# Attention scores in one-bank pieces from the top, products one step later, two transposed banks, and two gates halved

## The chip, the cores and the metric

The kernel runs on one core of a Trainium2 chip. The time is that of the device, in microseconds (us), from start to end of one launch; three runs of the kernel before gave 1307.58, 1307.06 and 1303.7, with the median at 1307.06. PE is the TensorE matrix engine, DVE is VectorE, ACT is ScalarE, POOL is GpSimd and SP is SyncE.

## What is computed

One layer of an encoder trunk on a sequence of 1024 tokens with 1024 channels, all in float32. Two token mixers (a pooling mixer over u and a stick-breaking attention over q, k, v) are merged by sigmoid gates, then an MLP with squared ReLU follows. The part on which the change bears:

```python
h = rmsnorm(x) * g_pre_mix
[u_pool | q | k | v] = h @ w_in
y_pool = multiscale_pool(u_pool) @ w_br_pool
y_sb   = stick_breaking_attention(q, k, v) @ w_br_sb       # 8 heads of 64
[g_pool | g_sb] = sigmoid(h @ w_gate + b_gate)
x = x + rmsnorm((g_pool * y_pool + g_sb * y_sb) @ w_out) * g_post_mix
x = x + rmsnorm(relu(rmsnorm(x) * g_pre_mlp @ w_up)**2 @ w_down) * g_post_mlp

def stick_breaking_attention(q, k, v):        # for each block of 128 queries t
    z = (qb @ kb.T) * scale
    mask = s < t                               # strictly causal
    log_1mb = where(mask, log_sigmoid(-z), 0)
    tail = cumsum(log_1mb, from the right) - log_1mb
    attn = where(mask, exp(log_sigmoid(z) + tail), 0)
    out = attn @ vb
```

So A[t,s] is sigmoid(z[t,s]) times the product of sigmoid(-z[t,j]) over all j between s and t.

## The kernel before, in words

**Precision.** A product of two float32 matrices is done as three matmuls of their high and low parts (hi x hi, lo x hi, hi x lo). `L112`, `L113` and `L114` are these three; a "dense step" is such a triple for one block of 128 input channels.

**The stages.** The input phase computes the two halves of the tokens' mean squares (`ms`, by a matmul with ones, L332), turns them into reciprocal roots `rb` (`rstd`: Ln L153 and Exp L154 on ACT, then L155 to L157 on DVE), transposes `rb` on PE (`rt`, L336) and copies a column of it into `rcol` (L337). Beside this run the products of u (`du`, `zu`: four groups, two halves each; L380 multiplies a finished half by `rb` and so frees its bank), the pooling mixer (`dm`), q and k of the first heads, and the first half of v. Then come attention, the merge of the branches, and the MLP.

**Attention.** Eight heads; each has eight rows of 128 queries, done in the order 6, 7, 4, 5, 2, 3, 0, 1. `att_scores` does one row i, which is w = 128(i+1) keys wide: the scores z on PE (L544, L547), T = sigmoid(z) and F = sigmoid(-z) on ACT (L551, L552), POOL zeroes T above the diagonal (L554), DVE replaces F by its running product from the right (the scan, L559) and multiplies T by it (L560). `att_out` does a pair of rows g: for each of its g+1 steps m, PE transposes four 128x128 blocks of T (`at`, L576), ACT rounds them to `ahi` (L583), DVE keeps the rest in `alo` (L584), and PE multiplies v by both into `o` (L589). At the end of the pair ACT and DVE add up the two halves of `o` into `oT` (L593, L594).

**What sets the order.** Each engine runs its instructions in a fixed order. `fill` lists, for each head, dense work that is put between the rows and steps (gates `dg`, later q and k `dqk`, the second half of v `dv`): `pump` hands out dense steps by a credit, `w_out` after each step's transpositions and a share of the rest after each row. A gate has two halves of 8 steps, so head 4 has 32 dense steps, heads 5 and 6 have 48 each. Within this, the framework's scheduler orders the instructions, and `marks` pin some of them. Head h's pair g is transposed while the next pair's scores are made.

**Banks.** The accumulators of PE lie in 8 banks: two for dense work (`d`), two tiles of two banks for z (a row of up to 1024 scores), one for `o` and one for `at`. `ms` of the first half and both `rt` use the bank of `at`, `ms` of the second half that of `o`.

Of the kernel before, what the change touches and what calls it, by code (L numbers as in the profile page):

```python
# [29 lines left out]
P = 128  # L30
# [19 lines left out]
class Block:  # L50
# [118 lines left out]
    def build(self):  # L169
# [9 lines left out]
            3: [("q", 2), ("k", 2), ("v", 12, 32)],  # L179
            4: [("g", 3), ("g", 11)],  # L180
            5: [("q", 3), ("k", 3), ("g", 4)],
            6: [("g", 12), ("g", 5), ("g", 13)],
            7: [("g", 6), ("g", 14), ("g", 7)],
# [64 lines left out]
    def phase_in(self):  # L248
# [81 lines left out]
        def stats(h):  # L330
            ms = self.zps.tile([P, H], F32, name="ms", tag="at" if h == 0 else "o", bufs=1)
            nc.tensor.matmul(ms, self.ones, accs[h], start=True, stop=True)  # L332
            self.rstd(ms, pa, ("sq", 3), out=self.rb[h])
            rt = self.zps.tile([P, H], F32, name="rt", tag="at", bufs=1)
            for j in range(4):
                nc.tensor.transpose(rt[:, j * P : j * P + P], self.rb[h][:, j * P : j * P + P], self.eye)  # L336
            nc.vector.tensor_copy(  # L337
                self.rcol[:, 4 * h : 4 * h + 4].rearrange("p (j o) -> p j o", o=1),
                rt.rearrange("p (j o) -> p j o", o=P)[:, :, 0:1],
            )  # L340

        z0 = self.zps.tile([P, 1024], F32, name="zu0", tag="z", bufs=2)
        z1 = self.zps.tile([P, 1024], F32, name="zu1", tag="z", bufs=2)
        d2 = [self.dps.tile([P, H], F32, name="du", tag="d") for _ in range(2)]
        dst = [d2] + [[z[:, h * H : h * H + H] for h in range(2)] for z in (z0, z1)]
        gens = [self.dense_steps(dst[g][0], self.weights(("u", g), 0), self.hT[0]) for g in range(3)]
# [60 lines left out]
        def pool_mix(g, cur):  # L407
# [6 lines left out]
            for h in range(2):  # L414
                c = slice(h * H, h * H + H)
                d = self.zps.tile([P, H], F32, name="dm", tag=("o", "at")[h], bufs=1)
                self.mm3(d, [(wmh[:, g, :], wml[:, g, :], ph[:, c], pq[:, c])])
# [110 lines left out]
    def att_scores(self, h, i):  # L528

        nc = self.nc
        p, j = h // 2, h % 2
        q, qs, k = self.qk[("q", p)][j], self.qk[("qs", p)][j], self.qk[("k", p)][j]
        w = (i + 1) * P
        z = self.zps.tile([P, 1024], F32, name="z", tag="z", bufs=2)
        pieces = [(0, max(256, min(H, w)))]
        if w > H:  # L540
            pieces.append((H, max(256, w - H)))
        tt = slice(i * P, i * P + P)
        for c, n in pieces:
            m = nc.tensor.matmul(z[:, c : c + n], q[:, tt], k[:, c : c + n], start=True, stop=False)  # L544
            if c == 0:
                self.marks.append(m)
            nc.tensor.matmul(z[:, c : c + n], qs[:, tt], k[:, c : c + n], start=False, stop=True)  # L547
        odd = i // 2 % 2
        tl = self.tp.tile([P, 1024 if odd else 768], F32, name="T", tag=f"T{odd}", bufs=2)
        f = self.tp.tile([P, 1024], F32, name="F", tag="F", bufs=1)  # L550
        nc.scalar.activation(tl[:, :w], z[:, :w], AF.Sigmoid)  # L551
        nc.scalar.activation(f[:, :w], z[:, :w], AF.Sigmoid, scale=-1.0)  # L552
        fr = f[:, w - 1 :: -1]
        nc.gpsimd.affine_select(  # L554
            out=tl[:, w - P : w], in_=tl[:, w - P : w], pattern=[[-1, P]], compare_op=ALU.is_gt, fill=0.0, base=0,
            channel_multiplier=1,
        )
        past = self.past[:, 1024 - w :][:, ::-1]
        nc.vector.tensor_tensor_scan(fr, fr, past, 1.0, ALU.mult, ALU.max)  # L559
        nc.vector.tensor_mul(tl[:, : w - 1], tl[:, : w - 1], f[:, 1:w])  # L560
        return tl

    def att_out(self, h, g, a):

        nc = self.nc
        o = self.zps.tile([P, 256], F32, name="o", tag="o", bufs=1)
        hd = (h % 4) * P
        for m in range(g + 1):
            diag = m == g
            at = self.zps.tile([P, H], F32, name="at", tag="at", bufs=1)  # L570
            hi = self.tp.tile([P, H], F32R, name="ahi", tag="ahi", bufs=2)
# [12 lines left out]
            nc.vector.tensor_sub(lo[:, c0:], at[:, c0:], hi[:, c0:].bitcast(F32))  # L584
            for part in (hi, lo):
                for s, c in ((2 * m + 1, 0), (2 * m, 256)):
                    v = self.v[(h // 4, s)].rearrange("p h x -> p (h x)")[:, hd : hd + P]
                    first = m == 0 and c == 0 and part is hi
                    t = nc.tensor.matmul(o, v, part[:, c : c + 256], start=first, stop=diag and c == 256 and part is lo)  # L589
            self.marks.append(t)  # L590
        b = 64 * (h % 2)
# [21 lines left out]
    def phase_attention(self):  # L613
# [5 lines left out]
        self.credit, self.queue = 0.0, []  # L619
        self.w_out = 2.3  # L620
        self.pin = True
        self.cut = 512
# [32 lines left out]
        self.w_out = 8.0  # L655
        self.att_out(*prev)
        while self.queue:
            self.advance()
# [645 lines left out]
```

## Time and profile before

| | before |
|---|---|
| runs | 1307.58, 1307.06, 1303.7 us |
| profiled execution | 1308.59 us |
| its span (first to last instruction) | 1306.8 us |
| attention, by its `at` and `o` rows | about 97 to 502 us |
| mean granted clock of PE | 0.993 |

A row of the timeline reads: start, duration, engine, line, operation, what it writes and reads, shape, how many were merged, and in brackets how long the engine stood idle before it and what ended the wait. A window's row reads: the stretch, its length, then for PE, PE's weight loads, DVE, ACT and POOL the busy time and number of instructions, then PE's granted clock as a share, the DMA engines' busy share and GB/s. Rows of groups end in the busy time, the mean duration in ns, and the idle time before them.

### The profile page before, as it was taken

The page shows a single profiled execution, that of the slowest core. Times are in us where ns is not written, and L with a number is a line of the kernel's source. Part 1 is how long each engine was busy: PE and PEld are TensorE (multiplying, and loading weights), DVE is VectorE, ACT ScalarE, POOL GpSimd, SP SyncE. Part 2 cuts the span into 40 slices and gives each one's busy share as a digit, 9 for nine tenths or more (in the row PEclk, how much of TensorE's full clock was granted, in tenths as well). Part 3 has the DMA queues.
Part 4 walks back from the last instruction along what each step waited for, and adds up shares of the span by engine and source line. Part 5 has one row for each costly group of instructions (what it writes and reads, how often), then busy time and mean ns, then how long its engine had stood idle before and what let it go on. Part 6 is the DMA issues. An engine that isn't in the chain of part 4 may idle for free.

```text
span 1306.8 us, 16746 instructions
## 1 busy us (share of the span) xinstructions
PE 1278.9 (98%) x6145; PEld 1066.9 (82%) x6145; DVE 915.6 (70%) x1239; ACT 600.7 (46%) x925; POOL 173.8 (13%) x346
## 2 busy tenths in 40 slices
PE   9999999998999999999999999999999999999996
PEld 6888888887888888888878878888888888888886
DVE  8785587676777765663586869877775655776976
ACT  7244455544555543223355646544465433344341
POOL 1002213201212331100001001211121000001100
PEclk9998999999999999999999999999999999999998
DMA  6243635623746979543156667765559555556741
GB/s 221 71 155 113 204 103 155 136 66 73 154 147 191 251 230 240 166 170 104 54 188 229 189 227 251 251 229 184 188 211 354 180 185 202 193 178 240 241 166 65
DMA packets 75746, 233.72 MB, mean 179 GB/s; under 512 B 8624, under 2 KB 11184, under 8 KB 73488
## 3 DMA queue, kind: packets, MB, share of 16 engines
q1 hardware_dynamic: 47936, 143.64, 33.5%
q0 software_dynamic: 27152, 88.49, 22.7%
q8 instruction: 48, 0.79, 0.2%
q10 hardware_dynamic: 576, 0.52, 0.1%
q14 instruction: 34, 0.28, 0.1%
HBM read 178.10 MB, written 83.89 MB: 200 GB/s over the span
## 4 chain that ended last, share of the span: by engine, by line
PE 84%; DVE 8%; ACT 3%; DMA 2%; issue 2%; POOL 1%; SPq 0%; DVEq 0%; ACTq 0%; POOLq 0%
PE d L113 19%; PE d L114 19%; PE d L112 19%; PE dg L110 4%; PE dg L113 4%; PE dg L114 4%; PE o L589 2%; PE at L576 2%; DVE F L559 2%; DVE T L560 1%; PE dqk L114 1%; PE dqk L113 1%; DMA yscr<-win 1%; PE z L547 1%; PE z L544 1%
## 5 line engine op out<-in xcount | busy, mean ns | idle before, releaser
L113 PE MATMUL d<-blo,whi 128*128 128x512 f32 (+1 forms) x456 | 172.7, 379 | 0.0
L114 PE MATMUL d<-bhi,wlo 128*128 128x512 f32 (+1 forms) x456 | 171.9, 378 | 0.0
L112 PE MATMUL d<-bhi,whi 128*128 128x512 f32 (+1 forms) x456 | 168.6, 378 | 0.0
L559 DVE TENSOR_TENSOR_SCAN F<-F,past 128x896 f32<-128x896 f32 (+3 forms) x64 | 87.6, 1369 | 46.9 <-ACT F L552 46.5
L82 ACT CAST whi<-wraw 128x512 fp32r<-128x512 f32 (+1 forms) x88 | 67.6, 797 | 86.4 <-PE d L113 37.5
L110 PE MATMUL dg<-hT_hi,whi 128*128 128x512 f32 x256 | 105.3, 411 | 0.0
L114 PE MATMUL dg<-hT_hi,wlo 128*128 128x512 f32 x256 | 101.0, 394 | 0.0
L113 PE MATMUL dg<-hT_lo,whi 128*128 128x512 f32 x256 | 100.7, 393 | 0.0
L83 DVE TENSOR_TENSOR wlo<-wraw,whi 128x512 fp32r<-128x512 f32 (+1 forms) x88 | 77.8, 907 | 30.5 <-ACT whi L82 30.3
L114 PEld LDWEIGHTS d<-bhi,wlo 128*128 128x128 f32 x456 | 85.8, 188 | 16.1 <-issue 0.2
L113 PEld LDWEIGHTS d<-blo,whi 128*128 128x128 f32 x456 | 85.7, 188 | 16.1 <-issue 0.2
L112 PEld LDWEIGHTS d<-bhi,whi 128*128 128x128 f32 x456 | 85.5, 188 | 16.1
L584 DVE TENSOR_TENSOR alo<-at,ahi 128x512 fp32r<-128x512 f32 (+1 forms) x80 | 50.3, 629 | 43.2 <-ACT ahi L583 42.5
L113 PE MATMUL d<-b_lo,whi 128*128 128x512 f32 x196 | 76.7, 392 | 0.0
L112 PE MATMUL d<-b_hi,whi 128*128 128x512 f32 x196 | 75.7, 391 | 0.0
L114 PE MATMUL d<-b_hi,wlo 128*128 128x512 f32 x196 | 75.3, 392 | 0.1
L1071 DVE TENSOR_TENSOR wlo<-slots_hi,whi 128x1024 fp32r<-128x1024 f32 x29 | 35.5, 1225 | 53.8 <-ACT whi L1069 53.8
L1069 ACT CAST whi<-slots_hi 128x1024 fp32r<-128x1024 f32 x29 | 30.5, 1052 | 84.6 <-PE d L113 64.7
L583 ACT CAST ahi<-at 128x512 fp32r<-128x512 f32 (+1 forms) x80 | 43.5, 544 | 47.5 <-PE at L576 44.2
L1069 ACT CAST whi<-slots_lo 128x1024 fp32r<-128x1024 f32 x27 | 28.4, 1052 | 72.9 <-PE d L113 59.2
L1071 DVE TENSOR_TENSOR wlo<-slots_lo,whi 128x1024 fp32r<-128x1024 f32 x27 | 33.0, 1222 | 36.7 <-ACT whi L1069 36.7
L114 PEld LDWEIGHTS dg<-hT_hi,wlo 128*128 128x128 f32 x256 | 48.3, 189 | 10.5
(305 smaller groups left out, 3325.9 us busy)
## 6 DMA issues: line engine op xcount, KB each, us to landing
wraw<-w SPq DMA_DIRECT2D x80, 512.0 KB, 4.2
wscr<-w POOLq DMA_DIRECT2D x24, 1024.0 KB, 10.3
ext_b<-ascr SPq DMA_DIRECT2D x40, 512.0 KB, 4.4
gscr<-gs POOLq DMA_DIRECT2D x32, 256.0 KB, 4.1
gate<-gscr POOLq DMA_DIRECT2D x16, 512.0 KB, 3.7
pscr<-p SPq DMA_DIRECT2D x32, 256.0 KB, 3.6
braw<-w SPq DMA_DIRECT2D x16, 512.0 KB, 5.5
ascr<-c POOLq DMA_DIRECT2D x32, 256.0 KB, 5.1
```

The lines of the kernel that those rows point to most:

```text
L82: nc.scalar.copy(hi[:, c], raw[:, c])
L83: self.last_lo = nc.vector.tensor_sub(lo[:, c], raw[:, c], hi[:, c].bitcast(F32)).ins
L110: nc.tensor.matmul(ps, wh, rh, start=first and i == 0, stop=False)
L112: nc.tensor.matmul(ps, wh, rh, start=first and i == 0, stop=False)
L113: nc.tensor.matmul(ps, wh, rl, start=False, stop=False)
L114: nc.tensor.matmul(ps, wl, rh, start=False, stop=last and i == n - 1)
L559: nc.vector.tensor_tensor_scan(fr, fr, past, 1.0, ALU.mult, ALU.max)
L576: t = nc.tensor.transpose(at[:, b * P : b * P + P], a[tt][:, s * P : s * P + P], self.eye)
L583: nc.scalar.copy(hi[:, c0:], at[:, c0:])
L584: nc.vector.tensor_sub(lo[:, c0:], at[:, c0:], hi[:, c0:].bitcast(F32))
L1069: last_split[0] = nc.scalar.copy(hi, src).ins
L1071: last_split[1] = nc.vector.tensor_sub(lo, src, hi.bitcast(F32)).ins
```

## The change

Scores: a row is done in pieces of at most 512 keys, the rightmost piece first. Each piece has a one-bank tile of z out of three (before: a two-bank tile out of two), its own F and T activations (F first), its own scan, which is seeded with the last value of the piece to its right, and its own multiplication. Products: `att_out` no longer multiplies a step's transposed blocks at once. It keeps them in `self.pending`, and `att_products` does them after the next step's transpositions have been issued; `at` gets two banks for it. The statistics' `ms` and `rt` of both halves all go to the single bank of `o`, the fourth `zu` and the second `dm` to the banks of `at`. Gates 4 and 12 are cut in halves between heads 4, 5 and 6, which now have 40, 48 and 40 dense steps. After the last pair the remaining dense steps are pumped ahead of the last products.

```diff
--- before.py
+++ after.py
@@ -177,9 +177,9 @@
             1: [("q", 1), ("k", 1), ("g", 9)],
             2: [("g", 2), ("g", 10), ("v", 0, 12)],
             3: [("q", 2), ("k", 2), ("v", 12, 32)],
-            4: [("g", 3), ("g", 11)],
-            5: [("q", 3), ("k", 3), ("g", 4)],
-            6: [("g", 12), ("g", 5), ("g", 13)],
+            4: [("g", 3), ("g", 11), ("g", 4, 0)],
+            5: [("g", 4, 1), ("q", 3), ("k", 3), ("g", 12, 0)],
+            6: [("g", 12, 1), ("g", 5), ("g", 13)],
             7: [("g", 6), ("g", 14), ("g", 7)],
             8: [("g", 15)],
         }
@@ -328,10 +328,10 @@
                     nc.vector.tensor_add(acc, acc, sq)
 
         def stats(h):
-            ms = self.zps.tile([P, H], F32, name="ms", tag="at" if h == 0 else "o", bufs=1)
+            ms = self.zps.tile([P, H], F32, name="ms", tag="o", bufs=1)
             nc.tensor.matmul(ms, self.ones, accs[h], start=True, stop=True)
             self.rstd(ms, pa, ("sq", 3), out=self.rb[h])
-            rt = self.zps.tile([P, H], F32, name="rt", tag="at", bufs=1)
+            rt = self.zps.tile([P, H], F32, name="rt", tag="o", bufs=1)
             for j in range(4):
                 nc.tensor.transpose(rt[:, j * P : j * P + P], self.rb[h][:, j * P : j * P + P], self.eye)
             nc.vector.tensor_copy(
@@ -339,10 +339,10 @@
                 rt.rearrange("p (j o) -> p j o", o=P)[:, :, 0:1],
             )
 
-        z0 = self.zps.tile([P, 1024], F32, name="zu0", tag="z", bufs=2)
-        z1 = self.zps.tile([P, 1024], F32, name="zu1", tag="z", bufs=2)
         d2 = [self.dps.tile([P, H], F32, name="du", tag="d") for _ in range(2)]
-        dst = [d2] + [[z[:, h * H : h * H + H] for h in range(2)] for z in (z0, z1)]
+        zu = [self.zps.tile([P, H], F32, name="zu", tag="z", bufs=3) for _ in range(3)]
+        zu.append(self.zps.tile([P, H], F32, name="zu", tag="at", bufs=2))
+        dst = [d2, zu[:2], zu[2:]]
         gens = [self.dense_steps(dst[g][0], self.weights(("u", g), 0), self.hT[0]) for g in range(3)]
         for k in range(NK):
             for g in gens:
@@ -413,7 +413,7 @@
             nc.vector.tensor_sub(pq, cur, ph.bitcast(F32))
             for h in range(2):
                 c = slice(h * H, h * H + H)
-                d = self.zps.tile([P, H], F32, name="dm", tag=("o", "at")[h], bufs=1)
+                d = self.zps.tile([P, H], F32, name="dm", tag=("o", "at")[h], bufs=h + 1)
                 self.mm3(d, [(wmh[:, g, :], wml[:, g, :], ph[:, c], pq[:, c])])
                 nc.scalar.activation(cur[:, c].bitcast(F32R), d, AF.Copy, scale=sc)
                 nc.vector.scalar_tensor_tensor(
@@ -535,39 +535,44 @@
         p, j = h // 2, h % 2
         q, qs, k = self.qk[("q", p)][j], self.qk[("qs", p)][j], self.qk[("k", p)][j]
         w = (i + 1) * P
-        z = self.zps.tile([P, 1024], F32, name="z", tag="z", bufs=2)
-        pieces = [(0, max(256, min(H, w)))]
-        if w > H:
-            pieces.append((H, max(256, w - H)))
-        tt = slice(i * P, i * P + P)
-        for c, n in pieces:
-            m = nc.tensor.matmul(z[:, c : c + n], q[:, tt], k[:, c : c + n], start=True, stop=False)
-            if c == 0:
-                self.marks.append(m)
-            nc.tensor.matmul(z[:, c : c + n], qs[:, tt], k[:, c : c + n], start=False, stop=True)
         odd = i // 2 % 2
         tl = self.tp.tile([P, 1024 if odd else 768], F32, name="T", tag=f"T{odd}", bufs=2)
         f = self.tp.tile([P, 1024], F32, name="F", tag="F", bufs=1)
-        nc.scalar.activation(tl[:, :w], z[:, :w], AF.Sigmoid)
-        nc.scalar.activation(f[:, :w], z[:, :w], AF.Sigmoid, scale=-1.0)
-        fr = f[:, w - 1 :: -1]
-        nc.gpsimd.affine_select(
-            out=tl[:, w - P : w], in_=tl[:, w - P : w], pattern=[[-1, P]], compare_op=ALU.is_gt, fill=0.0, base=0,
-            channel_multiplier=1,
-        )
-        past = self.past[:, 1024 - w :][:, ::-1]
-        nc.vector.tensor_tensor_scan(fr, fr, past, 1.0, ALU.mult, ALU.max)
-        nc.vector.tensor_mul(tl[:, : w - 1], tl[:, : w - 1], f[:, 1:w])
+        tt = slice(i * P, i * P + P)
+        past = self.past[:, 1024 - w :]
+        for c in range((w - 1) // H * H, -1, -H):
+            n = min(H, w - c)
+            top = c + n == w
+            cols = slice(c, c + max(256, n))
+            z = self.zps.tile([P, H], F32, name="z", tag="z", bufs=3)
+            zz = z[:, : max(256, n)]
+            m = nc.tensor.matmul(zz, q[:, tt], k[:, cols], start=True, stop=False)
+            if top:
+                self.marks.append(m)
+            nc.tensor.matmul(zz, qs[:, tt], k[:, cols], start=False, stop=True)
+            nc.scalar.activation(f[:, c : c + n], z[:, :n], AF.Sigmoid, scale=-1.0)
+            nc.scalar.activation(tl[:, c : c + n], z[:, :n], AF.Sigmoid)
+            if top:
+                nc.gpsimd.affine_select(
+                    out=tl[:, w - P : w], in_=tl[:, w - P : w], pattern=[[-1, P]], compare_op=ALU.is_gt, fill=0.0,
+                    base=0, channel_multiplier=1,
+                )
+
+            fr = f[:, c : c + n][:, ::-1]
+            nc.vector.tensor_tensor_scan(
+                fr, fr, past[:, c : c + n][:, ::-1], 1.0 if top else f[:, c + n : c + n + 1], ALU.mult, ALU.max
+            )
+            e = c + n - top
+            nc.vector.tensor_mul(tl[:, c:e], tl[:, c:e], f[:, c + 1 : e + 1])
         return tl
 
     def att_out(self, h, g, a):
 
         nc = self.nc
         o = self.zps.tile([P, 256], F32, name="o", tag="o", bufs=1)
-        hd = (h % 4) * P
         for m in range(g + 1):
             diag = m == g
-            at = self.zps.tile([P, H], F32, name="at", tag="at", bufs=1)
+            at = self.zps.tile([P, H], F32, name="at", tag="at", bufs=2)
             hi = self.tp.tile([P, H], F32R, name="ahi", tag="ahi", bufs=2)
             lo = self.tp.tile([P, H], F32R, name="alo", tag="alo", bufs=2)
             for b, (s, tt) in enumerate(((2 * m + 1, 0), (2 * m + 1, 1), (2 * m, 0), (2 * m, 1))):
@@ -582,12 +587,26 @@
                 nc.gpsimd.memset(lo[:, 0:P].bitcast(F32), 0.0)
             nc.scalar.copy(hi[:, c0:], at[:, c0:])
             nc.vector.tensor_sub(lo[:, c0:], at[:, c0:], hi[:, c0:].bitcast(F32))
-            for part in (hi, lo):
-                for s, c in ((2 * m + 1, 0), (2 * m, 256)):
-                    v = self.v[(h // 4, s)].rearrange("p h x -> p (h x)")[:, hd : hd + P]
-                    first = m == 0 and c == 0 and part is hi
-                    t = nc.tensor.matmul(o, v, part[:, c : c + 256], start=first, stop=diag and c == 256 and part is lo)
-            self.marks.append(t)
+            self.att_products()
+            self.pending = (h, g, m, o, hi, lo)
+
+    def att_products(self):
+
+        nc = self.nc
+        if self.pending is None:
+            return
+        h, g, m, o, hi, lo = self.pending
+        self.pending = None
+        diag = m == g
+        hd = (h % 4) * P
+        for part in (hi, lo):
+            for s, c in ((2 * m + 1, 0), (2 * m, 256)):
+                v = self.v[(h // 4, s)].rearrange("p h x -> p (h x)")[:, hd : hd + P]
+                first = m == 0 and c == 0 and part is hi
+                t = nc.tensor.matmul(o, v, part[:, c : c + 256], start=first, stop=diag and c == 256 and part is lo)
+        self.marks.append(t)
+        if not diag:
+            return
         b = 64 * (h % 2)
         u = self.sp.tile([P, 256], F32, name="ou", tag="ou", bufs=1)
         nc.scalar.copy(u[64:128, :], o[64:128, :])
@@ -618,6 +637,7 @@
         self.sp = tc.alloc_tile_pool(name="att_s", bufs=1, **kw)
         self.credit, self.queue = 0.0, []
         self.w_out = 2.3
+        self.pending = None
         self.pin = True
         self.cut = 512
         prev = None
@@ -654,6 +674,8 @@
             self.advance()
         self.w_out = 8.0
         self.att_out(*prev)
+        self.pump(self.w_out)
+        self.att_products()
         while self.queue:
             self.advance()
         self.pin = False
```

Some places show how this moves instructions. First, PE in the input phase. Before, at the second half's `ms` (it stands among products of the second group of u):

```order
L112 MATMUL zu_331<-hT_hi_290,whi 128x512
L113 MATMUL zu_331<-hT_lo_291,whi 128x512
L332 MATMUL ms<-acc,ones 128x512
L114 MATMUL zu_331<-hT_hi_290,wlo 128x512
L112 MATMUL zu_331<-hT_hi_290,whi 128x512
L113 MATMUL zu_331<-hT_lo_291,whi 128x512
L114 MATMUL zu_331<-hT_hi_290,wlo 128x512
L336 MATMUL rt<-eye,rb_165 128x128 x4
```

and at the second half's `rt` (`rb_166`):

```order
L113 MATMUL zu_332<-hT_lo_291,whi 128x512
L114 MATMUL zu_332<-hT_hi_290,wlo 128x512
L336 MATMUL rt<-eye,rb_166 128x128 x4
L112 MATMUL du<-hT_hi_249,whi 128x512
L113 MATMUL du<-hT_lo_250,whi 128x512
L114 MATMUL du<-hT_hi_249,wlo 128x512
```

The same place in the changed kernel:

```order
L113 MATMUL zu<-hT_lo_291,whi 128x512
L114 MATMUL zu<-hT_hi_290,wlo 128x512
L112 MATMUL zu<-hT_hi_290,whi 128x512
L332 MATMUL ms<-acc,ones 128x512
L113 MATMUL zu<-hT_lo_291,whi 128x512
L114 MATMUL zu<-hT_hi_290,wlo 128x512
L336 MATMUL rt<-eye,rb_166 128x128 x4
L112 MATMUL du<-hT_hi_249,whi 128x512
L113 MATMUL du<-hT_lo_250,whi 128x512
L114 MATMUL du<-hT_hi_249,wlo 128x512
```

The second `ms` has moved from the 30th row ahead of the second `rt` to the third.

Second, ACT at the start of attention, before (z_871 is row 6, 896 wide, z_883 row 7):

```order
L496 ACTIVATE v0_3_1040<-dv_1015,rcol_167 128x4x64
L551 ACT_TABLE_LOAD
L551 ACTIVATE T_876<-z_871 128x896
L552 ACTIVATE F_877<-z_871 128x896
L551 ACTIVATE T_888<-z_883 128x1024
L496 ACTIVATE v0_2_1068<-dv_1043,rcol_167 128x4x64
L496 ACTIVATE v0_1_1096<-dv_1071,rcol_167 128x4x64
L552 ACTIVATE F_889<-z_883 128x1024
```

and in the changed kernel (F_874 and T_873 are row 6, F_891 and T_890 row 7):

```order
L496 ACTIVATE v0_3_1052<-dv_1027,rcol_167 128x4x64
L553 ACT_TABLE_LOAD
L553 ACTIVATE F_874<-z_875 128x384
L554 ACTIVATE T_873<-z_875 128x384
L553 ACTIVATE F_874<-z_883 128x512
L554 ACTIVATE T_873<-z_883 128x512
L496 ACTIVATE v0_2_1080<-dv_1055,rcol_167 128x4x64
L553 ACTIVATE F_891<-z_892 128x512
L554 ACTIVATE T_890<-z_892 128x512
L553 ACTIVATE F_891<-z_900 128x512
L554 ACTIVATE T_890<-z_900 128x512
```

The first activation after the table's load is now 384 wide and is F, and each row's T follows its F by pieces.

Third, PE in head 4, before, at the scores of rows 2 (384 wide) and 3 (512 wide):

```order
L576 MATMUL at<-eye,T 128x128 x3
L544 MATMUL z<-k_2595,q_2467 128x384
L547 MATMUL z<-k_2595,qs_2588 128x384
L544 MATMUL z<-k_2595,q_2467 128x512
L547 MATMUL z<-k_2595,qs_2588 128x512
L589 MATMUL o<-ahi,v_1_2939 128x256
L589 MATMUL o<-ahi,v_0_2979 128x256
L589 MATMUL o<-alo,v_1_2939 128x256
L589 MATMUL o<-alo,v_0_2979 128x256
L576 MATMUL at<-eye,T 128x128 x4
L110 MATMUL dg<-hT_hi_290,whi 128x512
```

and at the same rows in the changed kernel:

```order
L549 MATMUL z<-k_2665,q_2527 128x384
L552 MATMUL z<-k_2665,qs_2658 128x384
L549 MATMUL z<-k_2665,q_2527 128x512
L552 MATMUL z<-k_2665,qs_2658 128x512
L549 MATMUL z<-k_2665,q_2527 128x256
L552 MATMUL z<-k_2665,qs_2658 128x256
L581 MATMUL at<-eye,T 128x128 x3
L606 MATMUL o<-ahi,v_1_3014 128x256
L606 MATMUL o<-ahi,v_0_3057 128x256
L606 MATMUL o<-alo,v_1_3014 128x256
L606 MATMUL o<-alo,v_0_3057 128x256
L606 MATMUL o<-ahi,v_3_2894 128x256
```

Before, the scores of rows 2 and 3 are all that stands between three transpositions and their products. Now the products of an earlier step follow (o with v_1 here), and then those of the four transpositions (o with v_3) that stand, not shown, just ahead of six rows of dg and these scores; the three transpositions shown wait one step longer for theirs.

And PE at the end of attention, before (dbr is the first product of the branch merge, d the next):

```order
L112 MATMUL dbr<-yh_4805,whi 128x512
L589 MATMUL o<-ahi,v_1_2939 128x256
L589 MATMUL o<-ahi,v_0_2979 128x256
L113 MATMUL dbr<-yl_4807,whi 128x512
L589 MATMUL o<-alo,v_1_2939 128x256
L589 MATMUL o<-alo,v_0_2979 128x256
L114 MATMUL dbr<-yh_4805,wlo 128x512
L112 MATMUL dbr<-yh_4793,whi 128x512
L113 MATMUL dbr<-yl_4795,whi 128x512
L114 MATMUL dbr<-yh_4793,wlo 128x512
```

and now:

```order
L112 MATMUL dbr<-yh_4967,whi 128x512
L113 MATMUL dbr<-yl_4969,whi 128x512
L114 MATMUL dbr<-yh_4967,wlo 128x512
L606 MATMUL o<-ahi,v_1_3014 128x256
L606 MATMUL o<-ahi,v_0_3057 128x256
L606 MATMUL o<-alo,v_1_3014 128x256
L606 MATMUL o<-alo,v_0_3057 128x256
L112 MATMUL d<-yh_4955,whi 128x512
L113 MATMUL d<-yl_4957,whi 128x512
L114 MATMUL d<-yh_4955,wlo 128x512
```

The last four products of `o` stood inside dbr, with 13 more rows of it behind them; now they stand behind all of dbr, and the first d follows at once.

## The prediction

> **What bounds the kernel now.** First the page: its head, the busy times and the clock row (the span in 40 slices of 32.7 us).
>
> ```profile
> span 1306.8 us, 16746 instructions
> ...
> PE 1278.9 (98%) x6145; PEld 1066.9 (82%) x6145; DVE 915.6 (70%) x1239; ACT 600.7 (46%) x925; POOL 173.8 (13%) x346
> ...
> PEclk9998999999999999999999999999999999999998
> ...
> PE 84%; DVE 8%; ACT 3%; DMA 2%; issue 2%; POOL 1%; SPq 0%; DVEq 0%; ACTq 0%; POOLq 0%
> ```
>
> PE is busy for 98%, and the change leaves its matmuls as they are. So it can give back only PE's idle time and the time at a lower clock, and it can cost only by making new idle time. The second view is therefore the waits of PE and of its weight loads in the attention stretch (97 to 502 us: total, times, longest), with the busy times of that stretch (PE, PEld, DVE, ACT, POOL, clock).
>
> ```profile
> 97.00:502.00 405.00, 393.79 (x2142) 337.53 (x2142) 275.47 (x371) 200.64 (x361) 95.17 (x202) 0.99 0.58 153
> ...
> PE z L544 <- ACT F L552: 3.1, 4, 1.9
> ...
> PE at L576 <- DVE T L560: 2.3, 1, 2.3
> ...
> PE o L589 <- DVE oT L594: 0.5, 1, 0.5
> ...
> PEld o L589 <- DVE alo L584: 5.4, 13, 1.6
> ```
>
> PE idles 405 - 393.8 = 11.2 us there, and these rows name nearly all of it. The timeline shows where, first at the start of attention:
>
> ```profile
> 102.53 1.28 ACT L551 ACT_TABLE_LOAD   x1 [2.98 <-DMA yscr<-win]
> ...
> 105.60 0.50 PE L544 MATMUL z<-k,q 128*128 128x512 f32 x1 [0.81 <-ACT F L552]
> ...
> 106.53 1.16 POOL L554 TENSOR_SCALAR_AFFINE_SELECT T<-T 128x128 f32<-128x128 f32 x1 [1.43 <-ACT T L551]
> ...
> 107.70 1.09 DVE L560 TENSOR_TENSOR T<-T,F 128x895 f32<-128x895 f32 x1
> ...
> 108.84 0.47 PE L576 MATMUL at<-eye,T 128*128 128x128 f32 x1 [2.28 <-DVE T L560]
> ...
> 108.00:112.00 4.00, 3.16 (x14) 2.95 (x15) 3.63 (x4) 1.62 (x2) 1.43 (x1) 0.50 0.00 0
> 112.00:116.00 4.00, 4.00 (x21) 3.78 (x21) 3.44 (x6) 2.45 (x5) 0.32 (x1) 0.70 0.06 10
> ```
>
> One chain, sigmoid table, T, F, scan, multiplication, ends in the first transposition; PE stands 0.81 us and then 2.28 us, and then works at half clock. And in head 4:
>
> ```profile
> 319.60 0.50 PE L544 MATMUL z<-k,q 128*128 128x512 f32 x1 [1.86 <-ACT F L552]
> ...
> 320.17 0.41 PE L589 MATMUL o<-ahi,v 128*128 128x256 f32 x2
> ...
> 321.98 0.51 PE L589 MATMUL o<-alo,v 128*128 128x256 f32 x2 [1.39 <-DVE alo L584]
> ...
> 320.00:324.00 4.00, 2.61 (x13) 2.13 (x12) 3.00 (x4) 0.62 (x2) 0.00 (x0) 0.83 1.08 199
> 324.00:328.00 4.00, 4.00 (x18) 3.37 (x18) 1.04 (x2) 1.18 (x3) 0.41 (x2) 0.75 0.02 4
> ```
>
> Here a score waits for a bank that F still reads, the products wait for alo, and the clock drops again. A wait costs more than its idle time: two 256-wide products take 0.24 us from 320.17, so PE could start again at 320.41, but starts at 321.98, 1.57 us for an idle of 1.39. I count 0.17 us more per wait.
>
> **What the change takes away.** (a) Products one step later. Between a step's transpositions and its products PE gets at least one whole step's work (order of PE: at least 3.7 us in its matmuls' durations, where 18 of the 80 steps had under 1.4 us). The chain transposition, ahi, alo takes about 2 us, so all waits on alo go: 5.4 + 13 x 0.17 = 7.6 us. The wait on oT goes too, 0.5 + 0.17 = 0.7. (b) Scores in pieces of one bank, three banks, F before T: a bank is free after two activations of half the width, and PE's order has mostly over 4 us of other work before a bank is used again. The z waits go: 3.1 + 4 x 0.17 = 3.8. (c) At the start of attention row 6 is ready about 3 us earlier: its first piece is 384 wide, and the order of ACT puts F first, so that the table (1.28 us) is loaded before the wait for the DMA, not behind it. The wait at 108.84 goes: 2.3 + 0.17 = 2.5. (d) The two clock drops follow idle sums of 0.81 + 2.28 and 1.86 + 1.39 us; without them they go. Half clock loses half the time: (1 - 0.70) x 4 and 0.50 x 3.16, 2.8 us, of which I take 2.5 since part of this stretch is the restart counted above; and (0.17 + 0.25) x 4 = 1.7. Together 4.2. All gains: 7.6 + 0.7 + 3.8 + 2.5 + 4.2 = **18.8 us**.
>
> **What it adds.** (e) The statistics in one bank. These rows are from the input phase, long before attention:
>
> ```profile
> 35.26 1.02 PE L332 MATMUL ms<-acc,ones 128*128 128x512 f32 x2
> ...
> 35.71 0.80 PE L114 MATMUL zu<-hT_hi,wlo 128*128 128x512 f32 x1
> ...
> 36.32 0.69 ACT L153 ACTIVATE rb<-ms,eps 128x512 f32<-128x512 f32 x1 [3.89 <-PE ms L332]
> ...
> 36.35 0.40 PE L112 MATMUL zu<-hT_hi,whi 128*128 128x512 f32 x1
> ...
> 36.59 0.40 PE L113 MATMUL zu<-hT_lo,whi 128*128 128x512 f32 x1
> ...
> 40.69 0.69 DVE L157 SCALAR_TENSOR_TENSOR rb<-nb,rb 128x512 f32<-128x512 f32 x1
> ...
> 41.30 1.28 DVE L380 TENSOR_TENSOR u<-du,rb 128x512 f32<-128x512 f32 x2
> ...
> 42.99 0.60 PE L336 MATMUL rt<-eye,rb 128*128 128x128 f32 x4
> ...
> 43.34 0.48 PE L112 MATMUL du<-hT_hi,whi 128*128 128x512 f32 x1
> ```
>
> The second half's mean square (ms, 35.26) starts a chain on ACT and DVE that ends with the second rb at 40.69 + 0.69 = 41.38, 6.12 us later, and PE transposes that rb at 42.99. Before, 29 rows of PE stand between ms and this transposition. The new order has ms two rows ahead of it, since ms now needs the bank of the first rt. The same work is ahead of the transposition as before, so PE reaches it at 42.99 again; from 35.26 to 36.35 PE did ms and one zu product (1.09 us), to 36.59 another (0.24), so ms starts 1.33 us before that, at 41.66; rb is ready at 41.66 + 6.12 = 47.78, and PE stands 4.8 us. Behind it du waits for the multiplication that frees its bank (half of the 1.28 us): about 48.45 instead of 43.34, **5.1 us**. Everything later, the DMA at 102.5 too, moves along with it. (f) An idle time longer than either of those before a clock drop should bring one: 1.7 to 2.8 us by the two in this trace, **2.2**; below it stands zero, if the gate's timing misses it.
>
> [...]
>
> (g) The end of attention. Before, dbr products stand between the last o and the phase that follows; the new order puts that phase's first product right behind the last o, whose bank it takes:
>
> ```profile
> 501.48 0.40 PE L589 MATMUL o<-alo,v 128*128 128x256 f32 x2
> ...
> 501.97 0.37 ACT L593 COPY ou<-o 64x256 f32<-64x256 f32 x1 [0.22 <-PE o L589]
> ...
> 502.37 0.42 DVE L594 TENSOR_TENSOR oT<-o,ou 64x256 f32<-64x256 f32 x1 [1.34 <-ACT ou L593]
> ```
>
> The two products take PE to 501.72, and oT ends at 502.79: **1.1 us** of waiting. (h) Twice as many activations, scans and multiplications in rows 4 to 7 of each head:
>
> ```profile
> L559 DVE TENSOR_TENSOR_SCAN F<-F,past 128x1024 f32<-128x1024 f32 x8 | 18.3, 2290 | 1.9 <-ACT F L552 1.7
> ...
> L559 DVE TENSOR_TENSOR_SCAN F<-F,past 128x512 f32<-128x512 f32 x8 | 9.8, 1222 | 2.2 <-ACT F L552 2.2
> ...
> L560 DVE TENSOR_TENSOR T<-T,F 128x1023 f32<-128x1023 f32 x8 | 9.8, 1224 | 0.4
> ...
> L560 DVE TENSOR_TENSOR T<-T,F 128x511 f32<-128x511 f32 x8 | 5.5, 686 | 0.2
> ...
> L552 ACT ACTIVATE F<-z 128x1024 f32<-128x1024 f32 x8 | 8.2, 1030 | 13.1 <-DVE T L560 12.9
> ...
> L552 ACT ACTIVATE F<-z 128x512 f32<-128x512 f32 x8 | 4.8, 595 | 4.1 <-DVE T L560 4.0
> ...
> 360.00:364.00 4.00, 4.00 (x22) 3.40 (x21) 3.97 (x6) 3.84 (x6) 0.90 (x1) 1.00 0.08 18
> ```
>
> A halved scan costs 2 x 1222 - 2290 = 154 ns more, a multiplication 148, so DVE gets 0.30 x 4 = 1.2 us more per head, and ACT 160 ns per activation x 8 = 1.3. The last row shows why this isn't free by itself: in the first half of a head DVE is full (3.97 of 4 us). What hides it is distance: from the last score of a row to its first transposition the new order of PE has mostly over 11 us of work (at least 5.6, in head 4). What hasn't room there: the select of the diagonal, which took 1160 ns beside a scan (106.53), delays the top multiplication. Bounds for all this: zero, if distance hides it, and 1.2 x 8 = 9.6 us if none of it is hidden; I take **1**, nearer to zero, since in this row PE is busy for 4.00 of 4 us beside a full DVE.
>
> [...]
>
> (i) Head 4 has 40 dense steps instead of 32, so PE has more to do while scores are prepared; following its new order with the durations of before leaves about **1.0 us** of waiting there.
>
> **The sum.** Losses: 5.1 + 2.2 + 1.1 + 1 + 1 = 10.4 us; net 18.8 - 10.4 = 8.4 us. The profiled execution took 1308.6 us (span 1306.8 and 1.8 around it), so 1300.2; the median of the runs shown lies 1.5 below it: **1298.7**.
>
> **Rivals.** First, the input phase doesn't stall: the new ms gets its bank early, or the chain to rb runs faster with nothing else on ACT and DVE, and the gain is 18.8 - 3.1 = 15.7: 1291.4. For it speaks that the chain's 6.12 us contain casts of weights (an rb instruction of 0.69 us is a small part); against it, that these casts stand in the new order as well, and that PE's order is fixed. Second, head 4 keeps its waits: its scores come from the same DVE, which is the engine that was late there. Its z and o waits and its clock drop cost about 8.4 us now, of which 1.0 is kept in the sum; were all but 1 kept, the time would be 1298.7 + 6.4 = 1305.1, within the 0.3% (about 3.9 us) that a measurement of this kernel can tell from no change. Against it stand 8 more dense steps and three banks. Third, slower: DVE becomes the bound in the first half of every head. Where the row above shows 3.97 of 4, the added 1.2 us and four selects that hold a top multiplication for 0.1 us each, 1.6 us per head, push rows 4 to 7 back until the transposition waits in each of the 8 heads: 13 us, 1311.7. It decides from the point where DVE's queue between a row's last score and its first transposition is longer than PE's work there; with 11 us against scans and multiplications of two rows, some 7 us, it isn't, except in head 4. Fourth, nothing happens because the single o bank takes the place of alo: a product would wait for the oT of the group before. That chain takes 1.1 us (above) and the new order has at least 2.6 us of PE's work in it, so I give it nothing of its own.
>
> **How the numbers follow.** Forecast 0.60, from 1294.5 (no clock drop, (h) and (i) at nothing) to 1303; no stall in the input phase 0.13; head 4 unchanged 0.15; DVE as the bound 0.12. The range 1291.0 to 1306.5 leaves out the third and part of the first rival. Faster by over 0.3% (below 1303.1): 0.57 + 0.13 + 0.02 = 0.72. Within 0.3%: 0.18. Slower (over 1311): 0.10.
>
> **What would show it.** In the waits of PE the rows on alo and F are gone or tiny, and the clock row has its full digit in the fourth slice. About 48 us after the start the transposition rt waits 4 to 5 us for DVE L157, with a clock under 1.00 in the windows behind it; if this wait is missing, (e) is wrong, if the clock stays at 1.00, (f). A wait of about 1 us for oT stands ahead of the first product after attention. If transpositions wait for the multiplication in several heads, (h) is wrong and the third rival is at work; if scores or transpositions wait in head 4 alone, it is the second.

## The result and the profile after

| | before | changed |
|---|---|---|
| median of 4 runs | 1306.34 us | 1290.47 us (1290.3 to 1291.31) |
| profiled execution, span | 1308.59, 1306.8 us | 1291.31, 1289.5 us |
| ratio to before | | 0.9882, 95% interval 0.9868 to 0.9896 |
| predicted | | 1298.7 us, range 1291.0 to 1306.5 |

The change saves 15.9 us, about twice what was forecast, and the time lies just under the range. First the page of the changed kernel, with the same lines as before: head, busy times, granted clock in 40 slices, chain that ended last.

```profile
span 1289.5 us, 16851 instructions
...
PE 1268.3 (98%) x6145; PEld 1063.1 (82%) x6145; DVE 924.2 (72%) x1303; ACT 605.5 (47%) x989; POOL 175.2 (14%) x346
...
PEclk9899999999999999999999999999999999999998
...
PE 88%; DVE 6%; DMA 2%; issue 2%; ACT 1%; SPq 0%; POOL 0%; DVEq 0%; POOLq 0%; ACTq 0%
```

The digit below 9 has moved from the fourth slice to the second: the clock now drops in the input phase and no longer at the start of attention. Next the waits of PE in the whole span (total, times, longest), and the busy times of the attention stretch (PE, PEld, DVE, ACT, POOL, clock).

```profile
PE rt L336 <- DVE rb L157: 4.6, 1, 4.6
...
PE d L112 <- DVE oT L613: 0.9, 1, 0.9
```

```profile
97.00:495.00 398.00, 396.80 (x2225) 344.59 (x2224) 288.61 (x442) 211.35 (x432) 99.47 (x205) 1.00 0.61 162
```

No row on alo, F or T is left; PE idles 1.2 us of 398, 0.9 of it at the very end, where it idled 11.2 of 405 before. The stall of the input phase is there as predicted, in the timeline and in windows of it (the clock is the third number from the end):

```profile
41.40 1.02 PE L332 MATMUL ms<-acc,ones 128*128 128x512 f32 x2
...
46.70 0.69 DVE L157 SCALAR_TENSOR_TENSOR rb<-nb,rb 128x512 f32<-128x512 f32 x1
...
47.45 1.11 PE L336 MATMUL rt<-eye,rb 128*128 128x128 f32 x4 [4.55 <-DVE rb L157]
48.21 0.77 PE L112 MATMUL du<-hT_hi,whi 128*128 128x512 f32 x1
```

```profile
44.00:48.00 4.00, 0.55 (x3) 0.55 (x4) 3.82 (x6) 0.61 (x2) 0.00 (x0) 0.72 0.38 102
48.00:50.00 2.00, 2.00 (x7) 1.68 (x6) 2.00 (x4) 0.00 (x0) 0.00 (x0) 0.50 0.14 57
50.00:52.00 2.00, 2.00 (x6) 1.54 (x5) 2.00 (x5) 0.00 (x0) 0.00 (x0) 0.50 0.00 0
52.00:54.00 2.00, 2.00 (x8) 1.57 (x8) 2.00 (x4) 0.00 (x0) 0.00 (x0) 0.84 0.00 0
```

At the start of attention, row 6's second multiplication ends at 111.16 and its transposition starts only at 114.88, with products of v and scores ahead of it and no idle time:

```profile
110.48 0.68 DVE L566 TENSOR_TENSOR T<-T,F 128x512 f32<-128x512 f32 x1
...
114.88 0.38 PE L581 MATMUL at<-eye,T 128*128 128x128 f32 x2
```

To see where the 17.3 us between the two profiled executions lie, I matched the traces by PE's own work: each matmul counts by its width, as one start follows another in these traces (0.227 us for 512 columns, 0.175 for 384, 0.120 for 256, 0.06 for a transposition), and rows with the same sum ahead of them are compared. The last column is the changed kernel's time minus that of before.

| time before, us | place | changed minus before |
|---|---|---|
| 40.0 | input phase, ahead of the stall | -0.7 |
| 47.3 | behind the second rt | +6.9 |
| 88.2 | ahead of attention | +6.8 |
| 114.7 | first transpositions done | +0.3 |
| 286.3 | heads 1 to 3 | -3.9 |
| 310.1, 338.4 | head 4, its middle and end | -6.7, -13.9 |
| 488.2 | last head | -16.4 |
| 508.5, 529.3 | first products of the merge, later ones | -15.3, -16.1 |
| 793.1 to the end | MLP | -17.4 |

So the input phase loses about what the sum said (7.3): PE comes 6.9 us late, and the stall itself is 7.6, since PE was 0.7 us ahead at 40 us. Attention gains 23.2 us up to 488 where the sum had 18.8 - 2 = 16.8.

### The profile page after: what moved, and what is told of

The parts are those of the page before. It is cut to its first block, busy times and chain, and to the rows that moved or that the text cites. A ratio compares the mean times of both kernels' runs of the same rounds, so it can differ in the third digit from the quotient of the medians.

```text
span 1289.5 us, 16851 instructions
## 1 busy us (share of the span) xinstructions
PE 1268.3 (98%) x6145; PEld 1063.1 (82%) x6145; DVE 924.2 (72%) x1303; ACT 605.5 (47%) x989; POOL 175.2 (14%) x346
## 4 chain that ended last, share of the span: by engine, by line
PE 88%; DVE 6%; DMA 2%; issue 2%; ACT 1%; SPq 0%; POOL 0%; DVEq 0%; POOLq 0%; ACTq 0%
PE d L114 18%; PE d L112 18%; PE d L113 18%; PE dg L110 5%; PE dg L114 5%; PE dg L113 5%; PE o L606 3%; PE at L581 2%; PE dqk L113 2%; PE dqk L114 2%; PE dqk L110 2%; DMA wraw<-w 2%; PE z L552 1%; PE z L549 1%; DVE wlo L83 1%
## 5 line engine op out<-in xcount | busy, mean ns | idle before, releaser
L562 DVE TENSOR_TENSOR_SCAN F<-F,past 128x384 f32<-128x384 f32 (+3 forms) x96 | 93.5, 974 | 25.8 <-ACT F L553 24.9
L112 PEld LDWEIGHTS d<-bhi,whi 128*128 128x128 f32 x456 | 85.5, 188 | 15.9
L553 ACT ACTIVATE F<-z 128x384 f32<-128x384 f32 (+3 forms) x96 | 47.3, 493 | 64.1 <-DVE T L566 38.4
L566 DVE TENSOR_TENSOR T<-T,F 128x127 f32<-128x127 f32 (+4 forms) x96 | 53.1, 556 | 10.2 <-POOL T L556 4.2
```

Of the source, the lines that this page charges most:

```text
L112: nc.tensor.matmul(ps, wh, rh, start=first and i == 0, stop=False)
L553: nc.scalar.activation(f[:, c : c + n], z[:, :n], AF.Sigmoid, scale=-1.0)
L562: nc.vector.tensor_tensor_scan(fr, fr, past[:, c : c + n][:, ::-1], 1.0 if top else f[:, c + n : c + n + 1], ALU.mult, ALU.max)
L566: nc.vector.tensor_mul(tl[:, c:e], tl[:, c:e], f[:, c + 1 : e + 1])
```

## Experiments

Chips differ by up to 1.5 us in the kernel before (medians of 1306.34 to 1307.86 us), so variants are compared by their ratios to the kernel before on their own chip; 0.0010 is 1.3 us, and the intervals are about 0.0015 to either side (0.0010 to 0.0023), so that a difference of two variants below some 0.002 can't be told from none. The changed kernel's is 0.9882.

**The stall of the input phase alone.**

```diff
-            ms = self.zps.tile([P, H], F32, name="ms", tag="o", bufs=1)
+            ms = self.zps.tile([P, H], F32, name="ms", tag=("o", "at")[h], bufs=h + 1)
```

> The changed kernel (1290.5 us), with the second half's ms in the free second bank of at instead of behind rt in the bank of o. Theory (the stall of the input phase costs its 4.6 us of waiting, the late du and a stretch at half clock, and PE's delay there goes on to the end): the row rt <- DVE rb is gone, the clock stays at 1.00 between 45 and 60 us, and the time is 6.5 to 7 us lower, 1283.5 to 1284. Rival (the stall only stands ahead of another: PE comes 7 us earlier to the first scores and transpositions and waits there for the pooling mixer's DMA and the sigmoid table): the gain is under 3 us, over 1287.5, and new waits stand between 97 and 110 us.

1284.79 us, 0.9825 [0.9810, 0.9839]: 0.0057, or 7.4 us, less than the changed kernel; matched like above, the two profiles differ by 4.9 us at rt, 7.4 behind the slow stretch, 7.0 all through attention and 6.8 at the end. From this run's timeline and one of its windows:

```profile
34.87 1.02 PE L332 MATMUL ms<-acc,ones 128*128 128x512 f32 x2
...
36.67 0.60 PE L336 MATMUL rt<-eye,rb 128*128 128x128 f32 x4
```

```profile
44.00:48.00 4.00, 4.00 (x19) 3.31 (x18) 4.00 (x7) 0.00 (x0) 0.00 (x0) 1.00 0.00 0
```

ms stands ahead of the first rt again, and PE works through 44 to 48 us at full clock. So nearly the whole price of sharing that bank is paid in the end time; what lies behind it takes back 0.6 us. This version beats both kernels.

**The end of attention.**

```diff
-        idle = self.zps.tile([P, H], F32, name="idle", tag="o", bufs=1)
+        idle = self.zps.tile([P, H], F32, name="idle", tag="z", bufs=3)
```

> The changed kernel, with the unread warm-up tile in a z bank, so that the banks of z and at, not that of o, are the first that the branch merge takes. Theory: the first product behind the last o no longer waits for oT; 1.0 to 1.2 us less than the changed kernel, 1289.3 to 1289.5. Rival: the wait moves to the next product that takes a bank of attention; no gain, 1290.2 to 1290.8.

1290.44 us, 0.9868 [0.9851, 0.9884]: not to be told from the changed kernel. The wait for oT is gone, but the waits of PE have a new row, about 280 us later (at 767.7 us, where oT was waited for at 489.2 in the changed kernel):

```profile
PE d L112 <- DVE u L1000: 0.9, 1, 0.9
```

With both edits:

> Both edits, the second ms in its own bank and o's bank not first. Theory: the two stalls are far apart on PE and add up, 7.5 to 8.2 us less than the changed kernel, 1282.3 to 1283. Rival: something off PE (DMA of weights into the branch merge) sets the end of attention, and only the larger of both gains shows, 1283.5 to 1284.

1284.87 us, 0.9825 [0.9810, 0.9840], the same as with the first edit alone. Its profile is 0.9 us shorter than that one's, and it has neither of these waits; in the times nothing of it can be seen. Whether the 0.9 us are taken back later in most executions stays open: the row on u stands in the next run too (0.6 us), beside a wait at the end of attention.

**Products at once.** The order of two lines in `att_out`:

```diff
-            self.att_products()
             self.pending = (h, g, m, o, hi, lo)
+            self.att_products()
```

> The changed kernel, with each step's products right behind its own transpositions again; pieces, banks and gates stay as changed. Theory (the delay of the products is what removed the waits on alo): the waits of o on alo come back, 7.6 + 0.7 us as the prediction had them and about 3 more for slow restarts that show no idle time, 1300 to 1303, and the o rows wait over 10 times. Rival (two transposed banks and pieces alone give PE enough to do): fewer than 5 waits on alo, under 1295.

1292.72 us, 0.9884 [0.9870, 0.9899]: the theory falls. Without the delay, too, no row on alo is left among PE's waits; the longest are these, the first in the input phase, the others at the end of attention, in the MLP and in attention:

```profile
PE rt L336 <- DVE rb L157: 4.6, 1, 4.6
...
PE d L112 <- ACT oh L719: 1.0, 1, 1.0
...
PE d L112 <- DVE u L1000: 0.6, 1, 0.6
...
PE dg L110 <- DVE v L497: 0.3, 1, 0.3
```

The order of PE says why: with a second bank of at free, the scheduler issues the next step's transpositions ahead of this step's products even where the code asks for the products first (at 59 of the 79 places where a step follows another; 1 before). PE's work between a step's transpositions and its products on alo, worked out from the order with the widths above, is at least 3.4 us here, at least 4.0 in the changed kernel, and under 2.05 at 19 of 80 steps before. The next three runs take the bank away or leave the delay alone.

**The delay alone, in the kernel before** (`att_products` and `self.pending` as in the change, everything else as before):

> The kernel before (1306 to 1308 us) with only the products one step later: whole rows, one bank of at, gates as before. Theory since the run with products at once (it is the second bank of at that puts distance between transpositions and products, the delay in the code does not): with one bank the next transpositions must wait for alo anyway, so the waits only change their place; within 0.3% of the kernel before, and o or at still wait some ten times. Rival (the prediction's own term: the delay is what removes them): 8 to 11 us less than the kernel before, no o row in the waits.

1307.01 us, 1.0006 [0.9996, 1.0016]: nothing. The waits are there under other names, in the attention stretch:

```profile
PE at L575 <- DVE alo L583: 6.8, 15, 0.9
PE at L575 <- DVE T L560: 2.3, 1, 2.3
PE o L600 <- DVE oT L607: 2.0, 5, 0.7
...
PE z L544 <- ACT F L552: 0.2, 1, 0.2
```

The next transposition now waits for alo to read the single bank, and products wait for oT, the fourth rival. The waits of z fell from 3.1 to 0.2 us, and the clock drop of head 4 is gone, but the new waits cost as much.

**One bank of at in the changed kernel**, with delayed products and then with products at once:

```diff
-            at = self.zps.tile([P, H], F32, name="at", tag="at", bufs=2)
+            at = self.zps.tile([P, H], F32, name="at", tag="at", bufs=1)
```

The fourth `zu` and the second `dm`, which lie in the same banks, get the one bank too.

> The changed kernel with one bank of at instead of two; pieces, delayed products and gates stay. Theory (second bank): most of what the prediction counted for the products comes back, 6 to 10 us more than the changed kernel, a ratio to the kernel before of 0.993 to 0.996, with waits of at or o for alo. Rival (pieces and delay suffice): within 2 us of the changed kernel, 0.987 to 0.990.

> The changed kernel with one bank of at and the products at once; pieces and gates stay. Theory (second bank): all of the waits of o on alo are back, 9 to 12 us more than the changed kernel, ratio 0.995 to 0.998; what is left against the kernel before is the start of attention, the score waits and the two clock drops, less the stall of the input phase. Rival (pieces alone): within 3 us of the changed kernel, ratio below 0.9905.

Both give 0.9962 (1301.34 us [0.9947, 0.9977] and 1301.51 [0.9949, 0.9975]): 0.0080, or 10.5 us, for the second bank with the delay, and 0.0078 without it, against the run with products at once, which differs from the second run in this bank alone; each of these differences is good to about 0.002, or 2.6 us. The kernel before uses eight banks, as the changed one does; a second bank of at without the pieces wasn't tried. With the delay the transpositions wait, as this row of the waits of the first shows; the rows below, of the second, have PE's own idle time and that of its weight loads for the same products.

```profile
PE at L581 <- DVE alo L589: 5.9, 11, 1.6
```

```profile
PE o L606 <- DVE alo L589: 2.4, 7, 0.5
```

```profile
PEld o L606 <- DVE alo L589: 5.0, 11, 0.8
```

PE's own row in the kernel before, beside the row of its weight loads (5.4, 13) that the prediction shows:

```profile
PE o L589 <- DVE alo L584: 4.7, 9, 1.4
```

The expectation "all of the waits" was too strong for the second: fewer and shorter waits come back than there were before. What is left without the second bank, pieces and the third bank of z above all, shows in the matched traces: in head 4 (from 286 to 338 us of the trace before) the second run gains 7.8 us and the changed kernel 10.0.

**Gates whole again.**

```diff
-            4: [("g", 3), ("g", 11), ("g", 4, 0)],
-            5: [("g", 4, 1), ("q", 3), ("k", 3), ("g", 12, 0)],
-            6: [("g", 12, 1), ("g", 5), ("g", 13)],
+            4: [("g", 3), ("g", 11)],
+            5: [("q", 3), ("k", 3), ("g", 4)],
+            6: [("g", 12), ("g", 5), ("g", 13)],
```

> The changed kernel with gates 4 and 12 whole again (32, 48 and 48 dense steps in heads 4 to 6). Theory (the prediction's part on head 4: too little dense work there): 2 to 5 us more than the changed kernel, ratio 0.990 to 0.992, with new waits between 285 and 320 us. Rival (banks and pieces alone cured head 4, the halving does nothing): within 1 us, ratio 0.987 to 0.989.

1290.66 us, 0.9881 [0.9866, 0.9896]: the halving does nothing that can be measured. Head 4 has no wait with 32 dense steps either.

**T ahead of F** (the two activations swapped):

> The changed kernel with T ahead of F in each piece, as before the change. Theory (the prediction's start of attention: F first lets the table load before the DMA wait and the scan start earlier): a wait of 1 to 2 us for T or F comes back between 100 and 112 us, and 0.5 to 3 us more in all (each first scan starts one activation of 0.6 us later), ratio 0.9885 to 0.991. Rival (distance hides the order of two half activations everywhere): within 0.5 us, ratio 0.987 to 0.989.

1291.27 us, 0.9883 [0.9866, 0.9901]: the rival. One transposition waits 0.3 us for a multiplication and a product of dg 0.4 us longer for v (0.7 for 0.3); no other wait of PE in attention is new.

**More work for DVE.** An operation that leaves F as it is, in rows 4 to 7, once or twice per piece.

```diff
             nc.vector.tensor_mul(tl[:, c:e], tl[:, c:e], f[:, c + 1 : e + 1])
+            if i >= 4:
+                nc.vector.tensor_tensor(f[:, c : c + n], f[:, c : c + n], f[:, c : c + n], op=ALU.max)
```

> The changed kernel with one more DVE operation on F, which leaves its values as they are, behind each piece's multiplication in rows 4 to 7 (five of 512 and one each of 384, 256 and 128 columns, 4.7 us per head by the multiplications' durations, 37.7 in all, four times what the change added). Theory (the work of PE between a row's last score and its first transposition hides it): under 3 us more than the changed kernel, ratio below 0.9905. Rival (the prediction's third: DVE is full in the first half of a head and its work adds to the time): 20 to 38 us more, ratio 1.003 to 1.017, with transpositions that wait for the multiplication in each head.

1292.76 us, 0.9895 [0.9879, 0.9911]: 1.7 us for some 38 us of work, which the intervals can't tell from nothing, with one new wait inside attention:

```profile
PE o L608 <- DVE alo L591: 0.7, 1, 0.7
```

> The same with two more operations per piece, 9.4 us per head and 75 in all. Theory: the distance of some 11 us is used up in most heads, so that waits of transpositions for the multiplication begin, but only the part beyond the distance is paid: 10 to 40 us more than the changed kernel, ratio 0.996 to 1.02. Rival (DVE as the bound): 57 to 75 us more, ratio 1.03 to 1.045. If it is still under 5 us, DVE has far more room than its busy share in the first half of a head says.

1313.80 us, 1.0062 [1.0039, 1.0085]: 23.5 us for 75. The waits come where the first theory had them only in part, since DVE's queue also delays alo and, through F, the banks of z. Behind such waits the clock drops three more times in attention, for 3.4 us each, at 198, 293 and 420 us. The two longest rows of PE's waits in attention:

```profile
PE o L609 <- DVE alo L592: 5.5, 7, 1.6
PE z L549 <- ACT T L554: 3.6, 3, 1.5
```

Between once and twice lies the point from which the third rival decides; the change's own 9.6 us are far below it.

## Why the prediction was wrong

**(a) The products: the effect was right, the cause and the size were not.** The waits on alo went. But the step said that they go because products come one step later, and the runs put that at nothing (0.9884 without it against 0.9882, and 1.0006 alone); the second bank of at is what lets PE go on, and it is worth 10.5 us where the terms had 7.6 + 0.7. The waits that show were not priced too low: by the times from one start to the next, PE lost 7.8 us at its waits for products of o, where the sum, which took the row of the weight loads, had 8.3. The size was short because it had no term for delays that leave no gap. Taking all pairs of neighbouring products in attention where the trace shows no idle time between them, the second starts later than the first's width accounts for by 3.5 us in all before (211 pairs), and by 0.3 after (242). Most of that, 2.6 us, is a second alo product that starts up to 0.1 us late, at 27 places. At 17 of these the first one had itself started late; at the others no wait can be seen, and what delays the second stays open. The rest are delays of up to 0.14 us, which leave no gap in PE's rows, since the row of a 256-wide product lasts 0.28 us and the next starts 0.12 us after it.

**(b) The score waits** went, as said. Pieces alone, with one bank of at, have no z row among their waits.

**(c) The start of attention:** the wait went, but F first isn't the reason, since T first costs nothing. The trace shows other work of PE ahead of the transposition until 3.7 us after row 6 was ready. Pieces alone has no such wait either and the delay alone keeps it (2.3 us), so neither the second bank nor the delay is the reason; which other part of the edit puts that work there wasn't tried.

**(d) The two clock drops** went; 97 to 495 us has a mean of 1.00. In the two stretches at half clock PE's matmuls took 4.3 us more than their widths account for (2.7 and 1.6), so the size, 4.2, was right. The reading of the first drop was not: this window of the kernel before

```profile
104.00:108.00 4.00, 1.75 (x11) 1.26 (x9) 2.33 (x2) 3.19 (x5) 1.45 (x2) 0.95 0.00 0
```

has a mean clock of 0.95, so half clock began at about 107.6, inside the second wait and after 1.8 us of idle time, not after 3.09. Outside these stretches, pairs of dense products without idle time (dg, dv, dqk) lost 9.3 us against their widths before and 7.3 after: 2.0 us for which the sum had no term. The clock isn't the reason, since pieces alone, whose only stretch of low clock ahead of its last 40 us is the 6.8 us of the input phase, has 9.3 too; the cause stays open.

**(e), (f) The stall of the input phase** was right nearly to the digit: 4.55 us of waiting for 4.8, du at 48.21 for 48.45, the clock at 0.50 behind it, PE late by 6.9 us for 7.3. Taking it away gave 7.4 us. The first rival, whose time (1291.4) came closest to the measured one, is wrong all the same: the stall is there, and the gain came from elsewhere.

**(g) The end of attention:** a wait of 0.9 us was there for 1.1, but removing it can't be seen in the times.

**(h), (i) What was held back for DVE, ACT, POOL and head 4** (2 us) was hardly needed: 38 us of further DVE work cost 1.7, which can't be told from nothing, and PE's only wait inside attention is one of 0.3 us (dg for v), as there was one before (dv for v). The 1.0 us for head 4 and the 8 dense steps that were to soften it were both beside the point.

**The sum.** Between the profiles the change saves 17.3 us where the sum had 8.4. From start to start, what had been priced in attention gave 18.3 us for 18.8: the waits of o 7.8 for 8.3, of z 3.7 for 3.8, of at 2.4 for 2.5, and the clock 4.3 for 4.2. Of the 8.9 us missing, 4.9 are the delays without a gap (2.9 between products of o outside the slow stretches, 2.0 between dense products), 2.0 are (h) and (i), which cost nothing that shows, 0.4 is the input phase, and 2.0 lie behind 500 us: 1.2 in the MLP, where the profile of before has a wait of 0.9 us for weights (released by ACT L889) that the changed kernel's doesn't have, and 0.8 at the first products of the merge. Nothing shows that the change is the cause of these 2.0: the run with pieces alone has that wait for weights again, with 1.6 us. Less the 0.5 us by which the priced gains came out lower this makes 8.8; 0.1 us I can't place.

The step that failed is the pricing of the gains, (a) above all. Its cause was the second bank and not the delay, and its size 10.5 us and not 8.3. Each unknown cost got a range, but the gains were taken as exact from the idle times, and these leave out the delays that show no gap.

## What to carry to other kernels

When a scheduler may reorder, look for the resource that keeps it from doing so: here a second accumulator bank gave all that the products gained (10.5 of some 23 us), while the same order written into the code without it only renamed the waits. Price a removed wait by the start-to-start times of the instructions around it, those without a gap too, not by the idle time alone. And when buffers are dealt out anew, follow those of the small, early chains too: one statistics tile in a shared bank cost 7 us of the 23 that the rest brought.

## What the runs showed of the hardware

In these profiles the low clock came in stretches of two lengths. In the changed kernel the four windows from 44 us add up to 2 x (0.28 x 4 + 0.50 x 2 + 0.50 x 2 + 0.16 x 2) = 6.9 us at half clock; in the run with o's bank moved, behind the same stall, to 2 x (0.13 x 4 + 0.50 x 2 + 0.08 x 2) = 3.4:

```profile
44.00:48.00 4.00, 1.02 (x5) 1.02 (x6) 3.93 (x6) 0.15 (x1) 0.00 (x0) 0.87 0.40 131
48.00:50.00 2.00, 2.00 (x6) 1.55 (x6) 2.00 (x5) 0.00 (x0) 0.00 (x0) 0.50 0.00 0
50.00:52.00 2.00, 2.00 (x9) 1.65 (x8) 2.00 (x6) 0.00 (x0) 0.00 (x0) 0.92 0.00 0
```

Matched like above, the stall delays PE from 40 us on by 7.6 us in the first and 6.8 in the second, between programs that are alike up to there. The two drops before were 6.8 and 3.4 us long as well.

What goes with the length shows with all profiles side by side, from the times at which the granted clock changes and from PE's rows. Ahead of each kernel's last 40 us, eleven profiles have 15 such stretches. In the 3.4 us ahead of them PE had idled 1.6 to 3.4 us. Nine are 3.4 us long, and in these PE idled at most 0.6 us within the stretch; six are 6.8 us long, and in the first 3.4 us of these PE idled 0.7 to 1.7 us. So in these profiles a drop lasted 6.8 us where PE was still waiting well into it: for 1.25 us within the first drop of before and 1.65 us in the changed kernel, against none within the second drop of before, which lasted 3.4.

Ahead of both drops of the kernel before, 1.8 of 3.4 us were idle. In the changed kernel the clock is low from 48 - 2.2 = 45.8 us on, 2.9 us after PE's last product ended at 42.9, and all nine profiles of this stall show a drop.

DVE, busy for 3.97 of 4 us in a window of the first half of a head before, could take 4.7 us more per head in the changed kernel, 38 us in all, for 1.7 us that the intervals can't tell from nothing: a high busy share of an engine in a stretch was no sign that it was the bound there.
